# First modulation ahead of the sums of squares, half of the norm's low parts on POOL, and other shares and rounds in the mixing stages

## Chip, cores and metric

One core of a Trainium2 chip runs the whole program. The metric is device time in microseconds of one execution. PE is the matmul engine, DVE, ACT and POOL the three engines for elementwise work, SP the queue that issues most DMAs.

## What is computed

A two-layer backbone of a diffusion model over 256 context and 1024 latent tokens, width 1024. Per layer, cut to what matters:

```
mod = silu(c) @ ada_w[i] + ada_b[i]          # six parts of 1024: shift, scale, gate, twice; a latent and a context row
h   = rmsnorm(x, norm1_g[i]) * (1 + sc1) + sh1
z   = h @ w_in[i]                            # columns for S5, RWKV-7, retention, GLA
mix = concat(s5(z), rwkv7(z), ret(z), gla(z)) @ w_out[i]     # each scans forward and backward
x   = x + g1 * mix
h   = rmsnorm(x, norm2_g[i]) * (1 + sc2) + sh2
x   = x + g2 * (relu(h @ mlp_w1[i]) ** 2 @ mlp_w2[i])
```

## The kernel before, in words

**Matmuls.** Big products are split: each operand is a rounded high part and a low part (the rest), and a product is high × high, high × low and low × high. So each normed tile has a high part `hh` and a low part `hl` (`mh`, `ml` ahead of the output projection and the MLP), and each weight tile `w_hi` and `w_lo`. `Pe.matmul` (L161) records every matmul, so they all have that line. PE takes its instructions in the order in which they were issued, as every engine does.

**Blocks.** The 1280 tokens are three blocks, of 256 (context), 512 and 512 columns, taken in the order 1, 2, 0 (`BORDER`). Each is eight tiles `kt` of 128 rows.

**Start.** `layer` (L1605) for layer 0 loads the three blocks `x`, one DMA each. For each it runs `sumsq`: ACT and POOL square four tiles each (`n_q`), DVE adds them up in `n_qa` (one buffer), PE adds over the rows by a product with ones. Then `rstd`: DVE's `n_s`, logarithm and exponential on ACT with a table load each, and four DVE operations that refine the root `n_r`. Behind all three runs `ada` for the first part: 16 loads of 512 KB (`ada_w`, five buffers), 32 products with the two condition rows, four copies on ACT (`ada_r`), four transposes, and the sum `mod` on DVE. `modg` makes the scale.

**Norm.** `norm` (L1571 on) then makes for each tile `n_h` on DVE (L1580, three buffers), `hh` on ACT with the shift added (L1581) and `hl` on DVE (L1582). It serves norm1 of both layers and the norms ahead of the MLPs. The output projection's inputs are split at L1669 to L1675, where odd tiles' `ml` is already subtracted on POOL.

**Mixing stage.** Behind the projections and S5, three generators run merged: ada's remaining parts, RWKV, and retention followed by GLA. `merged` (L2004) asks the one whose PE cost so far, divided by its share, is least for its next step. The shares are `MW`: the first number, times the number of ada parts (three in layer 0, two in layer 1), is ada's, the second RWKV's, the third that of retention and GLA. The order in which steps are issued, with the framework's scheduler behind it, gives each engine's order.

RWKV works through ten pairs of chunks per layer (`Rwkv.run`, L635). Pair by pair, its first part makes products and stores them (`rw_TE`, `rw_TO` to `rw_S`, L514), loads them in another layout (`rw_B`, one buffer, L518), and inverts unit triangular blocks on POOL in 31 steps of two operations (`rw_tmp` L527, `rw_Yv` L528). The result goes to DRAM and back (L530, `rw_DT` L533) and the second part (`unit2`) uses it. `RL` holds two numbers per layer: a new pair starts every R rounds, and the second part of a pair comes LAT rounds after its first:

```
R, LAT = self.RL
while act or r <= R * (NCH - 1) + LAT:
    b, q = divmod(r - LAT, R)
```

GLA works chunk by chunk; for each, POOL makes 16 scaled copies `gl_L` (L807 to L810), which PE multiplies.

Of the kernel before, what the change touches and what calls it, by code (L numbers as in the profile page):

```python
# [7 lines left out]
F32 = mybir.dt.float32  # L8
F32R = mybir.dt.float32r
I32 = mybir.dt.int32  # L10
AF = mybir.ActivationFunctionType
OP = mybir.AluOpType
# [299 lines left out]
class Rwkv:  # L312
# [268 lines left out]
    def chain(self, u, act):  # L581

        k, nc = self.k, self.k.nc
        V, A, PE = nc.vector, nc.scalar, k.pe
        p, d, ES = u["p"], u["d"], u["ES"]
        need = p >= 2 or self.need_ctx
        Y = self.w.tile([128, 256], F32, name="rw_Y", bufs=3)
        for e in range(2):
            py = k.ps("ch")
            RHi, RHn = self.RH[d, e], self.RH[d, 1 - e]  # L590
            for h in range(4):
                PE.matmul(py[:, h * 64:h * 64 + 64], ES[:, e, h], RHi[:, h], start=True, stop=True)
            y3 = py[:, 0:256].rearrange("p (h v) -> p h v", h=4)
            st = slice(0, 64) if e == 0 else slice(64, 128)
            ys = slice(64, 128) if e == 0 else slice(0, 64)
            yt = slice(0, 64) if e == d else slice(64, 128)
            V.tensor_tensor(RHn[st], y3[st], bc(u["E"][st, :, None], [64, 4, 64]), op=OP.mult)
            if need:
                A.copy(Y[yt], py[ys, 0:256])
            yield  # L600
        if need:
            if p in self.seen:
                act.append([self.finish(p, Y), 0])
            else:
                nc.sync.dma_start(self.dY[p, :, 0], Y)
                self.seen.add(p)
# [28 lines left out]
    def run(self):  # L635


        R, LAT = self.RL
        order = [(p, (1 - p) if p < 2 else (11 - p)) for p in range(NCH)]
        pairs, act, r = [], [], 0  # L640
        while act or r <= R * (NCH - 1) + LAT:
            b, q = divmod(r - LAT, R)
            if q == 0 and 0 <= b < NCH:
                act += [[self.unit2(u, act), 0] for u in pairs[b]["us"]]
            b, q = divmod(r, R)
            if q == 0 and b < NCH:
                pairs.append(dict(n=b, us=[]))
                act += [[self.unit1(order[b][d], d, pairs[b]), 0] for d in range(2)]
            r += 1
            for a in list(act):  # L650
                if a[1] > 0:
                    a[1] -= 1
                    continue
                try:
                    a[1] = next(a[0]) or 0
                except StopIteration:
                    act.remove(a)
                yield
            for pr in pairs:
                if len(pr["us"]) == 2 and "DT" not in pr["us"][0]:  # L660
                    pr["us"].sort(key=lambda u: u["d"])
                    self.inv(pr)
# [782 lines left out]


BLK = ((0, 256), (256, 768), (768, 1280))
MW = ((8, 165, 60), (8, 165, 60))
RL = ((6, 11), (6, 11))
FG = ((1, 4, 7), (2, 5))  # L1450
LATB = (1, 2)
BORDER = (1, 2, 0)
# [6 lines left out]
class Net:  # L1459
# [110 lines left out]
    def norm(self, x, n, g, sh, cond, hh, hl, pool, r=None):  # L1570

        k, nc = self.k, self.k.nc
        if r is None:
            ps = self.sumsq(x, n, pool)
            yield
            r = self.rstd(ps, n, pool)
        for kt in range(8):
            h = pool.tile([128, 512], F32, name="n_h", bufs=3)[:, :n]
            b = sh[:, kt, cond:cond + 1]
            nc.vector.scalar_tensor_tensor(h, x[:, kt], g[:, kt, cond:cond + 1], r[:, :n], op0=OP.mult, op1=OP.mult)  # L1580
            nc.scalar.activation(hh[:, kt], h, AF.Identity, bias=b)  # L1581
            nc.vector.scalar_tensor_tensor(hl[:, kt], h, b, hh[:, kt].bitcast(F32), op0=OP.add, op1=OP.subtract)  # L1582
        yield

    def hblocks(self, pool, name, bs=BORDER):
# [14 lines left out]
    def layer(self, i):  # L1600
        k, nc, I = self.k, self.k.nc, self.I
# [7 lines left out]
        h = self.hblocks(hp, "h")  # L1609
# [3 lines left out]
        npool = self.pool(tag + "n", "right")  # L1613
        if i == 0:
            aw = self.pool("aw", "right")
            self.x, self.nr = [None] * 3, {}
            ad = self.ada(0, 0, aw, 5)
            for b in BORDER:
                c0, c1 = BLK[b]
                self.x[b] = npool.tile([128, 8, c1 - c0], F32, name=f"x0{b}")  # L1620
                nc.sync.dma_start(self.x[b], self.xd[b])
                self.nr[b] = self.rstd(self.sumsq(self.x[b], c1 - c0, npool, 2, 2), c1 - c0, npool, 3)
            run(ad)
            aw.release()
        g1 = self.modg(sm["n1"], mod[:, 8:16])
        for b in BORDER:
# [2 lines left out]
        if i > 0:  # L1629
# [16 lines left out]
                  self.brow(w, "rw_lnb", I["rw_ln_b"][i]), w, not last, self.mixout(w, "rw", 2))  # L1646
        rw.RL = RL[i]
        rw.setup()
        ad = [(i, 1), (i, 2)] + ([] if last else [(i + 1, 0)])
        aw, rww, rgw = MW[i]  # L1650
        merge(k, [(chain([self.ada(a, q, w, 2) for a, q in ad]), aw * len(ad)), (rw.run(), rww), (chain([self.ret_run(i, last), self.gla_run(i, last)]), rgw)])
# [8 lines left out]
        npool = self.pool(tag + "n2", "right")  # L1660
# [4 lines left out]
        for b in ob:  # L1665
            c0, c1 = BLK[b]
            n = c1 - c0
# [11 lines left out]
        h = mix  # L1679
        for b in ob:  # L1680
            n = BLK[b][1] - BLK[b][0]
# [338 lines left out]
def merge(k, gens):  # L2020
    run(merged(k, gens))
# [41 lines left out]
```

## Time and profile before

| | |
|---|---|
| median of 3 runs | 3906.94 us (3906.47 to 3907.89) |
| profiled execution | 3916.12 us, its span 3914.3 us, mean granted clock 0.927 |
| busy: PE, DVE, ACT, POOL | 3563.0, 2254.2, 1476.7, 1350.4 us |
| share of the span's chain: PE, DVE, DMA, POOL, ACT | 67, 10, 8, 7, 5% |

The kernel runs through stages one after the other: start and norm1 to 102 us, projections and S5 to 466, the mixing stage to 1056, output projection and MLP to 2106, and in the same sequence layer 1: norm1 to 2142, projections to 2498, mixing to 3046, the rest to 3914. In the MLPs PE is busy all the time; in the mixing stages every engine has gaps. Busy time of an engine counts only in a stage in which others wait for it.

### The profile page before, as it was taken

The page shows a single profiled execution, that of the slowest core. Times are in us where ns is not written, and L with a number is a line of the kernel's source. Part 1 is how long each engine was busy: PE and PEld are TensorE (multiplying, and loading weights), DVE is VectorE, ACT ScalarE, POOL GpSimd, SP SyncE. Part 2 cuts the span into 40 slices and gives each one's busy share as a digit, 9 for nine tenths or more (in the row PEclk, how much of TensorE's full clock was granted, in tenths as well). Part 3 has the DMA queues.
Part 4 walks back from the last instruction along what each step waited for, and adds up shares of the span by engine and source line. Part 5 has one row for each costly group of instructions (what it writes and reads, how often), then busy time and mean ns, then how long its engine had stood idle before and what let it go on. Part 6 is the DMA issues. An engine that isn't in the chain of part 4 may idle for free.

```text
span 3914.3 us, 61529 instructions
## 1 busy us (share of the span) xinstructions
PE 3563.0 (91%) x23156; PEld 2970.4 (76%) x23156; DVE 2254.2 (58%) x4722; ACT 1476.7 (38%) x2992; POOL 1350.4 (34%) x2697
## 2 busy tenths in 40 slices
PE   3999888988799999999997999898888799999996
PEld 1998756677687888888886887767777678888885
DVE  5876455677565444444447875555776564444446
ACT  3266334765433111211124266446664331112222
POOL 1541156676441111111111551276674421111122
PEclk9999988877799999999998999997877899999998
DMA  4445475632431111111103434563423411111111
GB/s 173 142 127 148 136 216 140 193 85 70 140 113 33 33 44 33 44 33 44 33 28 102 148 120 143 175 210 102 112 76 96 134 59 49 44 43 44 54 49 44
DMA packets 350873, 372.84 MB, mean 95 GB/s; under 512 B 75408, under 2 KB 295760, under 8 KB 350320
## 3 DMA queue, kind: packets, MB, share of 16 engines
q1 hardware_dynamic: 315232, 343.07, 29.1%
q10 hardware_dynamic: 35344, 25.83, 2.2%
q8 instruction: 183, 3.00, 0.3%
q14 instruction: 114, 0.93, 0.1%
HBM read 285.18 MB, written 83.63 MB: 94 GB/s over the span
## 4 chain that ended last, share of the span: by engine, by line
PE 67%; DVE 10%; DMA 8%; POOL 7%; ACT 5%; issue 3%; SPq 1%; ACTq 0%; DVEq 0%; POOLq 0%
PE psb L161 57%; PE psu L161 5%; POOL rw_tmp L527 2%; DMA ada_w<-in_ada_w_dram 2%; POOL rw_Yv L528 2%; DMA rw_B<-rw_S 2%; PE psfi L161 1%; PE pss L161 1%; DVE s_W L1157 1%; DVE n_qa L1552 1%; DMA rw_S<-rw_Yv 1%; PE psch L161 1%; PE psu L165 1%; DVE s_CA L1157 1%; DMA n_h<-z_mix 1%
## 5 line engine op out<-in xcount | busy, mean ns | idle before, releaser
L161 PE MATMUL psb<-hl,w_hi 128*128 128x512 f32 (+1 forms) x1800 | 665.8, 370 | 6.9 <-DVE hl L1582 6.9
L161 PE MATMUL psb<-hh,w_hi 128*128 128x512 f32 (+1 forms) x1800 | 666.0, 371 | 5.3 <-DVE n_s L1561 2.3
L161 PE MATMUL psb<-hh,w_lo 128*128 128x512 f32 (+1 forms) x1800 | 662.6, 369 | 0.0
L161 PE MATMUL psb<-mh,w_hi 128*128 128x512 f32 (+1 forms) x1616 | 604.3, 375 | 21.9 <-ACT w_hi L1475 21.9
L161 PE MATMUL psb<-mh,w_lo 128*128 128x512 f32 (+1 forms) x1616 | 599.1, 372 | 4.1 <-DVE w_lo L1478 3.6
L161 PE MATMUL psb<-ml,w_hi 128*128 128x512 f32 (+1 forms) x1616 | 601.8, 373 | 0.0
L1939 DVE SCALAR_TENSOR_TENSOR x<-psb,mod,x 128x512 f32<-128x512 f32 (+1 forms) x648 | 438.9, 689 | 271.3 <-PE psb L161 270.6
L1478 POOL TENSOR_TENSOR w_lo<-w_raw,w_hi 128x1024 fp32r<-128x1024 f32 x84 | 216.8, 2581 | 751.8 <-ACT w_hi L1475 632.1
L1961 DVE TENSOR_TENSOR hr<-hr 128x512 f32<-128x512 f32 (+1 forms) x162 | 151.7, 937 | 504.6 <-ACT hr L1960 504.6
L1960 ACT ACTIVATE hr<-psb 128x512 f32<-128x512 f32 (+1 forms) x162 | 88.7, 548 | 850.9 <-PE psb L161 850.6
L161 PEld LDWEIGHTS psb<-hl,w_hi 128*128 128x128 f32 x1800 | 342.1, 190 | 72.5 <-DVE hl L1582 12.7
L161 PEld LDWEIGHTS psb<-hh,w_hi 128*128 128x128 f32 x1800 | 342.2, 190 | 67.5 <-issue 4.0
L161 PEld LDWEIGHTS psb<-hh,w_lo 128*128 128x128 f32 x1800 | 341.5, 190 | 59.1 <-issue 0.7
L1963 POOL TENSOR_TENSOR hl<-hr,hh 128x512 fp32r<-128x512 f32 (+1 forms) x81 | 95.6, 1181 | 800.3 <-ACT hh L1962 527.8
L161 PEld LDWEIGHTS psb<-mh,w_hi 128*128 128x128 f32 x1616 | 306.8, 190 | 81.8 <-ACT w_hi L1475 23.1
L161 PEld LDWEIGHTS psb<-mh,w_lo 128*128 128x128 f32 x1616 | 306.8, 190 | 63.1 <-DVE w_lo L1478 5.0
L161 PEld LDWEIGHTS psb<-ml,w_hi 128*128 128x128 f32 x1616 | 306.9, 190 | 58.8 <-issue 1.8
L1475 ACT CAST w_hi<-w_raw 128x1024 fp32r<-128x1024 f32 (+1 forms) x208 | 212.9, 1042 | 274.2 <-PE psb L161 263.0
L527 POOL TENSOR_TENSOR rw_tmp<-rw_Yv,rw_B 128x60 f32<-128x60 f32 (+24 forms) x620 | 206.2, 333 | 185.8 <-DMA rw_B<-rw_S 98.6
L161 PE MATMUL psb<-w_lo,hh 128*128 128x256 f32 (+1 forms) x928 | 264.6, 286 | 1.8 <-DVE w_lo L1478 1.8
L161 PE MATMUL psb<-w_hi,hl 128*128 128x256 f32 (+1 forms) x928 | 264.2, 286 | 0.0
L161 PE MATMUL psb<-w_hi,hh 128*128 128x256 f32 (+1 forms) x928 | 263.5, 288 | 0.3 <-ACT w_hi L1475 0.3
(470 smaller groups left out, 6690.8 us busy)
## 6 DMA issues: line engine op xcount, KB each, us to landing
w_raw<-in_mlp_w_dram SPq DMA_DIRECT2D x128, 512.0 KB
ada_w<-in_ada_w_dram SPq DMA_DIRECT2D x96, 512.0 KB
w_raw<-in_w_in_dram SPq DMA_DIRECT2D x40, 512.0 KB
w_raw<-in_w_out_dram SPq DMA_DIRECT2D x32, 512.0 KB
rw_zin<-z_rw SPq DMA_DIRECT2D x20, 576.0 KB
rw_B<-rw_S SPq DMA_DIRECT2D x20, 512.0 KB
z_rw<-zm SPq DMA_DIRECT2D x14, 640.0 KB
x<-in_xT_dram SPq DMA_DIRECT2D x4, 2048.0 KB
```

Source lines behind the costliest of these rows:

```text
L161: return self.t.matmul(out, lhsT, rhs, **kw)
L165: return self.t.transpose(out, a, ident)
L527: eng.tensor_tensor(o, bc(Yv[:, 0:m, s:s + 1], [128, m, n]), bc(B[:, s:s + 1, s + 1:32], [128, m, n]), op=OP.mult)
L528: eng.tensor_tensor(Yv[:, 0:m, s + 1:32], Yv[:, 0:m, s + 1:32], o, op=OP.add)
L1157: T_ = lambda o, a, b, op: V.tensor_tensor(o, a, b, op=op)
L1475: nc.scalar.copy(hi[:, :n], raw[:, :n])
L1478: e.tensor_tensor(lo[:, :n], raw[:, :n], hi[:, :n].bitcast(F32), op=OP.subtract)
L1552: nc.vector.tensor_tensor(acc[:, :n], acc[:, :n], q[:, :n], op=OP.add)
L1939: V.scalar_tensor_tensor(xb[:, dt_], ps[:, :n], mod[:, 40 + dt_, cnd:cnd + 1], xb[:, dt_], op0=OP.mult, op1=OP.add)
L1960: A.activation(r[:, :n], ps[:, :n], AF.Relu)
L1961: V.tensor_tensor(r[:, :n], r[:, :n], r[:, :n], op=OP.mult)
L1963: (G if j else V).tensor_tensor(hl[:, j, :n], r[:, :n], hh[:, j, :n].bitcast(F32), op=OP.subtract)
```

## The change

Four edits.

1. `MW`: ada's share per part is 16, where it was 8, in both layers.
2. `RL`: a new pair of RWKV chunks starts every 5 rounds, where it was every 6; the second part stays 11 rounds behind.
3. `norm`: for odd tiles ACT adds the shift in place, ACT copies the high part, and POOL subtracts to get the low part. Even tiles stay as they were. In the whole program 88 tiles are normed by it, 64 of 512 columns and 24 of 256.
4. `layer`: for layer 0 the three blocks' loads are followed by ada's first part, and by the sums and roots of the three blocks behind it.

```diff
-MW = ((8, 165, 60), (8, 165, 60))
-RL = ((6, 11), (6, 11))
+MW = ((16, 165, 60), (16, 165, 60))
+RL = ((5, 11), (5, 11))
...
-            nc.scalar.activation(hh[:, kt], h, AF.Identity, bias=b)
-            nc.vector.scalar_tensor_tensor(hl[:, kt], h, b, hh[:, kt].bitcast(F32), op0=OP.add, op1=OP.subtract)
+            if kt % 2:
+                nc.scalar.activation(h, h, AF.Identity, bias=b)
+                nc.scalar.copy(hh[:, kt], h)
+                nc.gpsimd.tensor_tensor(hl[:, kt], h, hh[:, kt].bitcast(F32), op=OP.subtract)
+            else:
+                nc.scalar.activation(hh[:, kt], h, AF.Identity, bias=b)
+                nc.vector.scalar_tensor_tensor(hl[:, kt], h, b, hh[:, kt].bitcast(F32), op0=OP.add, op1=OP.subtract)
...
-                self.nr[b] = self.rstd(self.sumsq(self.x[b], c1 - c0, npool, 2, 2), c1 - c0, npool, 3)
             run(ad)
+            for b in BORDER:
+                n = BLK[b][1] - BLK[b][0]
+                self.nr[b] = self.rstd(self.sumsq(self.x[b], n, npool, 2, 2), n, npool, 3)
```

PE's order at the start of the program, before (a row is an engine's instruction with its line, what it writes and reads, and how often it stands there in a row; `psb` is a bank of PSUM):

```order
L161 MATMUL psb_107<-n_qa,c_ones 128x512
L161 MATMUL psb_144<-n_qa,c_ones 128x512
L161 MATMUL psb_181<-n_qa,c_ones 128x256
L161 MATMUL psb_216<-ada_w,condsl 2x512 x32
L165 MATMUL psb_287<-c_ident,ada_r 128x128 x4
L161 MATMUL psb_425<-hh_92,w_hi 128x512
```

And with the change:

```order
L161 MATMUL psb_111<-ada_w,condsl 2x512 x32
L165 MATMUL psb_182<-c_ident,ada_r 128x128 x4
L161 MATMUL psb_188<-n_qa,c_ones 128x512
L161 MATMUL psb_223<-n_qa,c_ones 128x512
L161 MATMUL psb_258<-n_qa,c_ones 128x256
L161 MATMUL psb_437<-hh_92,w_hi 128x512
```

The three sums over rows moved from ahead of ada's products to behind its transposes.

DVE's order around the modulation of layer 0 (`mod`), before, with the last of the third block's sum and root chain (`n_qa` to `n_r`) ahead of it:

```order
L1552 TENSOR_TENSOR n_qa<-n_qa,n_q_200 128x256
L1561 TENSOR_SCALAR n_s<-psb_181 128x256
L1564 TENSOR_TENSOR n_t<-n_r 128x256
L1565 TENSOR_TENSOR n_t<-n_t,n_s 128x256
L1566 TENSOR_SCALAR n_t<-n_t 128x256
L1567 TENSOR_TENSOR n_r<-n_r,n_t 128x256
L1531 TENSOR_TENSOR mod_75<-psb_287,small_73 128x32
L1539 SCALAR_TENSOR_TENSOR modg<-mod_75,small_73 128x16
L1580 SCALAR_TENSOR_TENSOR n_h<-x_105,modg,n_r 128x512 x3
L1582 SCALAR_TENSOR_TENSOR hl_93<-n_h,mod_75,hh_92 128x512 x2
```

And with the change, from the last add of the first block on:

```order
L1552 TENSOR_TENSOR n_qa<-n_qa,n_q_207 128x512
L1478 TENSOR_TENSOR w_lo<-w_raw,w_hi 128x1024 x3
L1531 TENSOR_TENSOR mod_75<-psb_182,small_73 128x32
L1539 SCALAR_TENSOR_TENSOR modg<-mod_75,small_73 128x16
L1561 TENSOR_SCALAR n_s<-psb_188 128x512
L1552 TENSOR_TENSOR n_qa<-n_qa,n_q_225 128x512
L1552 TENSOR_TENSOR n_qa<-n_qa,n_q_229 128x512
L1564 TENSOR_TENSOR n_t<-n_r 128x512
L1552 TENSOR_TENSOR n_qa<-n_qa,n_q_230 128x512
L1565 TENSOR_TENSOR n_t<-n_t,n_s 128x512
L1552 TENSOR_TENSOR n_qa<-n_qa,n_q_235 128x512
L1566 TENSOR_SCALAR n_t<-n_t 128x512
```

All three root chains, and the second and third block's adds, moved from ahead of the modulation to behind it, in between the norm's operations.

POOL's order at the end of the last inversion of layer 0, before (`gl_L` are a GLA chunk's copies, `rw_Y` to `gl_nth` the outputs' group norms):

```order
L809 TENSOR_TENSOR gl_L<-gl_c 128x8x8
L810 TENSOR_TENSOR gl_L<-gl_c 128x8x8
L528 TENSOR_TENSOR rw_Yv<-rw_Yv,rw_tmp 128x7x4
L527 TENSOR_TENSOR rw_tmp<-rw_Yv,rw_B 128x24
L528 TENSOR_TENSOR rw_Yv<-rw_Yv,rw_tmp 128x8x3
L527 TENSOR_TENSOR rw_tmp<-rw_Yv,rw_B 128x16
L528 TENSOR_TENSOR rw_Yv<-rw_Yv,rw_tmp 128x8x2
L527 TENSOR_TENSOR rw_tmp<-rw_Yv,rw_B 128x8
L528 TENSOR_TENSOR rw_Yv<-rw_Yv,rw_tmp 128x8
L624 TENSOR_TENSOR rw_Y<-rw_Y,rw_YQ 128x256
```

And with the change:

```order
L527 TENSOR_TENSOR rw_tmp<-rw_Yv,rw_B 128x8
L528 TENSOR_TENSOR rw_Yv<-rw_Yv,rw_tmp 128x8
L624 TENSOR_TENSOR rw_Y<-rw_Y,rw_YQ 128x256
L706 TENSOR_TENSOR rw_grs<-rw_gs,mhalf 128x4
L706 TENSOR_TENSOR gl_nrs<-gl_ns,mhalf 128x4
L624 TENSOR_TENSOR rw_Y<-rw_Y,rw_YQ 128x256
L706 TENSOR_TENSOR rw_grs<-rw_gs,mhalf 128x4
L724 TENSOR_TENSOR gl_nth<-gl_nth,gl_lng 128x256
L807 TENSOR_TENSOR gl_L<-gl_c 128x64
L808 TENSOR_TENSOR gl_L<-gl_c 128x64
L809 TENSOR_TENSOR gl_L<-gl_c 128x64
L810 TENSOR_TENSOR gl_L<-gl_c 128x64
```

The last GLA chunk's sixteen copies, which stood inside the inversion, come behind it. In layer 0 eight chunks' copies stood inside inversions and two between them; now six do, three stand between and one behind.

## Rows read from the trace of the kernel before

**Rows 1.** Stretches: each engine's busy us (instructions), PE's granted clock, DMA share, GB/s.

```profile
core 0: us, PE busy (x) PEld busy (x) DVE busy (x) ACT busy (x) POOL busy (x), PEclk, DMA share, GB/s
...
95.00:105.00 10.00, 10.00 (x53) 8.40 (x54) 9.64 (x38) 4.75 (x9) 0.00 (x0) 1.00 0.29 108
...
466.00:1056.00 590.00, 498.13 (x4986) 394.98 (x4986) 392.02 (x1037) 316.97 (x859) 367.64 (x1005) 0.81 0.49 140
1010.00:1037.00 27.00, 27.00 (x382) 24.02 (x386) 14.12 (x33) 9.92 (x25) 3.61 (x5) 0.72 0.15 45
2106.00:2133.00 27.00, 14.34 (x43) 9.85 (x43) 27.00 (x44) 18.39 (x25) 1.44 (x2) 0.68 0.57 175
2498.00:3046.00 548.00, 462.00 (x4438) 379.96 (x4438) 355.40 (x945) 295.78 (x802) 337.85 (x952) 0.79 0.44 129
```

**Rows 2.** PE's timeline, start: start us, length, instruction, count, [idle before, releaser].

```profile
49.13 1.22 PE L161 MATMUL psb<-n_qa,c_ones 128*128 128x256 f32 x2 [11.01 <-DVE n_qa L1552]
50.27 3.73 PE L161 MATMUL psb<-ada_w,condsl 128*2 128x512 f32 x20
...
69.13 1.03 PE L161 MATMUL psb<-ada_w,condsl 128*2 128x512 f32 x4 [0.26 <-DMA ada_w<-in_ada_w_dram]
72.74 1.05 PE L165 MATMUL psb<-c_ident,ada_r 128*128 128x128 f32 x4 [2.58 <-ACT ada_r L1524]
75.83 0.79 PE L161 MATMUL psb<-hh,w_hi 128*128 128x512 f32 x1 [2.03 <-ACT hh L1581]
```

**Rows 3.** DVE's timeline, start.

```profile
24.74 0.69 DVE L1561 TENSOR_SCALAR n_s<-psb 128x512 f32<-128x512 f32 x1 [2.17 <-PE psb L161]
...
33.49 0.68 DVE L1567 TENSOR_TENSOR n_r<-n_r,n_t 128x512 f32<-128x512 f32 x1
...
73.83 0.19 DVE L1531 TENSOR_TENSOR mod<-psb,small 128x32 f32<-128x32 f32 x1 [19.14 <-PE psb L165]
...
100.62 1.27 DVE L1582 SCALAR_TENSOR_TENSOR hl<-n_h,mod,hh 128x256 fp32r<-128x256 f32 x3
```

**Rows 4.** Tile rw_B's readers on POOL, 466 to 1056: ns min/median/max, first, last.

```profile
L527 POOL TENSOR_TENSOR rw_tmp<-rw_Yv,rw_B x310: 201/298/1347, 519.7 to 1003.0; 128x60 f32<-128x60 f32 x15, 128x54 f32<-128x54 f32 x10, 128x66 f32<-128x66 f32 x10, 128x28 f32<-128x28 f32 x10
```

**Rows 5.** POOL's timeline, an inversion of layer 0 and one of layer 1.

```profile
784.11 0.29 POOL L807 TENSOR_TENSOR gl_L<-gl_c 128x64 f32<-128x64 f32 x1 [1.46 <-DMA gl_c<-z_gk]
...
793.01 0.34 POOL L810 TENSOR_TENSOR gl_L<-gl_c 128x64 f32<-128x64 f32 x1
...
2951.90 0.38 POOL L807 TENSOR_TENSOR gl_L<-gl_c 128x64 f32<-128x64 f32 x1 [4.97 <-PE psb L161]
```

**Rows 6.** SP's timeline ahead of the inversion from 768.6 on.

```profile
750.71 0.83 SPq L514 DMA_DIRECT2D rw_S<-rw_TE  x2
...
758.00 0.57 SPq L518 DMA_DIRECT2D rw_B<-rw_S  x1
```

**Rows 7.** ACT's timeline, start.

```profile
12.56 0.63 ACT L1549 ACTIVATE n_qa<-x 128x512 f32<-128x512 f32 x1 [6.41 <-DMA x<-in_xT_dram]
...
24.74 0.63 ACT L1549 ACTIVATE n_qa<-x 128x512 f32<-128x512 f32 x1 [2.30 <-PE psb L161]
```

**Rows 8.** DVE in 2106 to 2133, by line: busy us, mean ns.

```profile
L1582 DVE SCALAR_TENSOR_TENSOR hl<-n_h,mod,hh 128x512 fp32r<-128x512 f32 x15 | 10.9, 746 | 0.0
```

**Rows 9.** POOL's timeline at the inputs of layer 0's output projection.

```profile
1063.51 1.26 POOL L1675 TENSOR_TENSOR ml<-n_h,mh 128x512 fp32r<-128x512 f32 x1 [12.30 <-ACT mh L1673]
```

**Rows 10.** DVE's timeline in the same place.

```profile
1062.79 0.69 DVE L1675 TENSOR_TENSOR ml<-n_h,mh 128x512 fp32r<-128x512 f32 x1 [10.65 <-ACT mh L1673]
1064.15 1.17 DVE L1675 TENSOR_TENSOR ml<-n_h,mh 128x512 fp32r<-128x512 f32 x1 [0.67 <-ACT mh L1673]
```

**Rows 11.** The page's costliest groups: busy us, mean ns, idle before.

```profile
L161 PE MATMUL psb<-ml,w_hi 128*128 128x512 f32 (+1 forms) x1616 | 601.8, 373 | 0.0
```

**Rows 12.** PE in 1010 to 1037, groups by line.

```profile
L161 PE MATMUL psb<-gl_L 32*32 32x32 f32 (+1 forms) x228 | 7.3, 222 | 0.0
```

**Rows 13.** Waits in 466 to 1056: total us, times, longest.

```profile
PE psfi L161 <- DMA ada_w<-in_ada_w_dram: 15.1, 5, 7.2
```

## The prediction

> **What bounds the kernel now.** I read the profile in this order: the busy times by stretch, the four engines' timelines at the start, the two norms, the POOL chain of the two mixing stages, and last the order of both kernels. The profiled execution took 3916.1 us, 9.2 above the median of the runs, 3906.9. I sum differences against it and carry the sum over to the median. About 0.2%, 7.8 us, is what a measurement can tell from no change.
>
> PE is the engine that counts, and it is short of work in a few places only. In 466 to 1056 and 2498 to 3046, the stages that mix RWKV, retention and GLA, it is busy 498 of 590 and 462 of 548 us; at the second norm1 it has 14.3 us of work in 27 while DVE is busy all of them [rows 1]. At the start it stands in order: its first ada matmul comes at 50.27, right behind the third sum of squares, and the first twenty then run without a wait, so five loads had been there for long. The other eleven follow at 1.29 us each to 69.13; transposes at 72.74, first projection at 75.83 [rows 2]. DVE sat idle for 19.1 us before the modulation at 73.83 and ends the norm at 101.9 [rows 3]. From 95 on PE has no gap [rows 1].
>
> The mixing stages hang on a chain on POOL: twenty inversions of 31 steps each, where the next pair's block is loaded into the one buffer that the last one frees. Ten of them run from 519.7 to 1003 in layer 0, some 48 us each, though a step is two operations of 0.3 us, some 20 us in all [rows 4]. The rest is the load, and other POOL work that stands between the steps. Two GLA chunks inside one inversion took 784.1 to 793.3, some 4.2 us each without the steps between, and in layer 1 the chain stood 5 us behind a GLA operation that waited for PE [rows 5]. The RWKV products that feed the load are there 7 us before it is issued [rows 6].
>
> **Start (ada's first part ahead of the sums).** No operation is removed. The x blocks' loads, 5 MB, are first on SP, then 16 ada loads with 5 of weights among them, 10.5 MB: 31 halves of a megabyte at 1.29 us, 40 us. The first 2 MB were there at 12.56 [rows 7], so the stream began at about 7.4 and the last ada load is there at 47. Its transposes end 4.7 us later, as now [rows 2], at 52, against 73.8. ACT's copies of ada's result and DVE's modulation now stand behind three casts and three low parts of weights; the loads of those are issued ahead of the eleventh ada load, so they are over by then. But now PE runs the three sums behind them. The buffer of sums is one: the second block's first square waits for the first sum on PE, as now at 24.74 [rows 7]. So the second and third sums and their root chains move behind the modulation, where the wait for ada hid them. From a sum's n_s to its n_r DVE and ACT need 9.4 us [rows 3]; the first normed tile starts at about 63, 11 us earlier than now.
>
> The norm's end decides, as PE takes the three blocks in turn. From 63 on DVE has 16 n_h and 8 hl of 512 columns at 0.73 [rows 8], 17.5; 12 of 256 at 0.42 [rows 3], 5; the third block's adds, 3; two root chains of five operations, 5: 30 us, or an end at 93. POOL has 8 subtracts of 1.26 [rows 9], four of half the size, 2.5, and four squares, 2.5: 15 us. If DVE stands still for all of those, the end is 108.
>
> Does it stand still? A subtract on DVE of two SBUF tiles took 0.69 alone and 1.17 when it started 0.64 us into a POOL subtract; it ended 0.55 after that one [rows 9, 10], so it lost 0.48 of the 0.62 us that POOL still needed, some 80%. Taken so, the norm ends at 63 + 30 + 12 = 105. PE has been running gapless since 95 on what was done, so some 3 us more than now cost nearly nothing: **+1 us, between −10 (no standstill) and +4 (full standstill)**.
>
> The Trainium skill (SBUF — State Buffer, "Who interferes with whom") speaks against this part of the change: a VectorE instruction with two SBUF inputs and a GpSimd one that reads SBUF share a port pair, and the second one waits for the whole instruction. By it the start would be +4 and the next term +4, the sum 5 us higher; the 1.17 us row agrees with a wait, a little short of a full one.
>
> **norm1 of layer 1 (the same subtracts).** DVE is the bound for the two large blocks, 27 of 27 us [rows 1]. A pair of tiles costs it 4 × 0.73 = 2.92 [rows 8]. With the odd subtract on POOL it is 2.19 with no standstill, 2.19 + 1.26 = 3.45 with a full one, 3.20 at 80%. Eight pairs: −6, +4, and I take **+2**. ACT's three operations of a pair, one more than now, take 1.9 us at the 0.63 of its square [rows 7], less than DVE's. The three n_h buffers hold: by these prices an odd tile keeps its own for 3.3 us and an even one for 2.1, together 1.8 us a pair. The norms ahead of the MLP cost **0**, ±2: no matmul ever waits for ml [rows 11], because the other blocks' work covers them; if that cover went, each would pay the 2 us of above.
>
> **Shares and rounds (the mixing stages).** Both edits only reorder. In POOL's order of layer 0, GLA chunks inside inversions go from 8 to 6: pair 5 loses both (−8.4 at 4.2 each [rows 5], and a wait), pair 6 gains one, pair 8 loses one, pair 4 gets small ones. Where a chunk stands while the load is under way it costs nothing. By pairs I get −10 for the chain; with the waits it could be −16, and if the moved work only makes others late 0. But one chunk's work now comes after the last inversion, and PE has 271 GLA matmuls instead of 162 behind its last pair. There it is busy 27 of 27 us at a granted clock of 0.72 [rows 1], 7.3 us of them on gl_L products alone [rows 12]; two thirds more of these and their like is +8. Net **−2**, from −14 to +12. In layer 1 one chunk leaves the second last inversion, −4.2 and perhaps the 5 us wait [rows 5], others move by a few us either way, and the tail is as before: **−4**, from −12 to +6. The ada loads come denser and all ahead of pair 4. PE's waits for them are 15.1 us in the whole stage [rows 13], ahead of products that are 7 us early: 0, within the ends above.
>
> **Sum.** +1 + 2 − 2 − 4 = −3: 3904 us. All lower ends together would be −44, all upper +28; they hardly meet.
>
> **Rivals.**
> *No standstill worth the name.* The 1.17 us may be one unlucky pair. Then the start gives −10 and norm1 −6, with −6 from the mixing stages: −22, 3885. For it: DVE was the one engine at work in both norms. Against it: the row itself.
> *The tails don't fill.* The clock of 0.72 rises to the 1.00 of other stretches and the extra GLA products fit in; the chains give −10 and −6, norms +3: −13, 3894.
> *Slower: the GLA backlog behind layer 0's last pair.* If the chain's end at 1003 doesn't come earlier, since the chunks taken out of inversion 5 return in 6 and 7, the +8 stays whole, and the last chunk's scores, their mask and norm on DVE follow in series, some 8 more; with +5 from the norms and −2 from layer 1 it is +19, 3926. It decides once the last inversion ends less than 8 us earlier. For it: PE is full there. Against: two chunks less in the chain.
> *The change does nothing where POOL bounds.* The load and the 31 steps are the same; then only the norms' +3 count: 3910, within the forecast's own case.
>
> **Chances.** Forecast with the last rival 0.38, no standstill 0.19, tails that fill 0.16, backlog 0.20, and 0.07 for larger losses of the same kind. Of the two faster rivals nearly all is faster by over 0.2% (0.34 after a little is taken off); the backlog and its like and a bit of the forecast give slower 0.28; same 0.38. The range 3880 to 3932 takes in the first rival at its low end and the backlog with 6 us to spare. The forecast's own range is 3897 to 3912.
>
> **What would show it.** Right: the first projection at 63 to 66 but the norm's end near 104; POOL's new subtracts at 1.2 to 1.3 us with n_h or hl beside them lengthened to over 1 us; DVE's stretch of the second norm1 2 us longer; ten inversions ending some 10 us earlier against the stage's start, and the stage shorter by much less. Wrong: a norm that ends at 93, DVE operations at their 0.73 beside POOL, a last inversion of layer 0 as late as now, or a stage that is shortened by all its chain gave.

## The result, and the profile after

The changed kernel took **3925.81 us** (median of 4 runs, 3919.04 to 3929.23), the kernel before 3906.7 beside it: ratio 1.0051, 95% interval 1.0032 to 1.0071. It is slower by 0.5%, where 3904 was forecast. The profiled execution is one of 3926.94 us, span 3925.1.

To compare stages I count PE's matmuls of projections, output projections and MLPs from the start of the program (their order is the same in all kernels here up to a few rows) and read when the n-th starts. "Start" ends at the 200th, layer 0's mixing stage lies between the 2200th and the 2400th, norm1 of layer 1 between the 7300th and the 9000th, layer 1's mixing stage between the 9400th and the 9600th. Two repeats with the identical order of matmuls (`n_dve1` of before, `n1a` of the change, below) give each kernel a second trace:

| us | before | its repeat | changed | its repeat | difference of means |
|---|---|---|---|---|---|
| start, to the 200th | 119.9 | 122.5 | 125.9 | 125.2 | +4.4 |
| layer 0's mixing stage | 647.6 | 640.7 | 644.3 | 642.3 | -0.9 |
| norm1 of layer 1 | 346.3 | 344.2 | 342.4 | 342.2 | -3.0 |
| layer 1's mixing stage | 602.2 | 593.9 | 610.0 | 605.9 | +9.9 |
| last matmul | 3893.1 | 3884.5 | 3903.3 | 3899.7 | +12.7 |

The other +2.3 are small parts of the MLPs and projections. Before's profiled execution, 9 us over its median, was long in the mixing stages: its repeat, with the same order, is 15.2 us shorter in these two and 6.6 longer elsewhere, 8.6 shorter in sum. "norm1 of layer 1" is a long stretch, since the end of layer 0's MLP lies in it too.

PE's timeline at the start of the changed kernel (columns as in [rows 2]):

```profile
48.86 1.03 PE L161 MATMUL psb<-ada_w,condsl 128*2 128x512 f32 x4 [1.74 <-DMA ada_w<-in_ada_w_dram]
52.47 1.09 PE L165 MATMUL psb<-c_ident,ada_r 128*128 128x128 f32 x4 [2.58 <-ACT ada_r L1524]
53.35 1.92 PE L161 MATMUL psb<-n_qa,c_ones 128*128 128x512 f32 x2
68.38 2.08 PE L161 MATMUL psb<-n_qa,c_ones 128*128 128x512 f32 x2 [13.12 <-DVE n_qa L1552]
84.11 1.22 PE L161 MATMUL psb<-n_qa,c_ones 128*128 128x256 f32 x2 [13.65 <-DVE n_qa L1552]
87.25 0.77 PE L161 MATMUL psb<-hh,w_hi 128*128 128x512 f32 x1 [1.92 <-DVE n_s L1561]
```

DVE's timeline there, and POOL's:

```profile
53.60 0.19 DVE L1531 TENSOR_TENSOR mod<-psb,small 128x32 f32<-128x32 f32 x1 [13.16 <-PE psb L165]
65.67 2.06 DVE L1580 SCALAR_TENSOR_TENSOR n_h<-x,modg,n_r 128x512 f32<-128x512 f32 x3
77.28 1.75 DVE L1580 SCALAR_TENSOR_TENSOR n_h<-x,modg,n_r 128x512 f32<-128x512 f32 x1
96.87 0.74 DVE L1580 SCALAR_TENSOR_TENSOR n_h<-x,modg,n_r 128x512 f32<-128x512 f32 x1
106.25 0.47 DVE L1587 SCALAR_TENSOR_TENSOR hl<-n_h,mod,hh 128x256 fp32r<-128x256 f32 x1
```

```profile
77.04 1.44 POOL L1584 TENSOR_TENSOR hl<-n_h,hh 128x512 fp32r<-128x512 f32 x1
```

The modulation comes at 53.6 (73.83 in [rows 3]) and the first normed tile at 65.67. But the first projection starts at 87.25, later than the 75.83 of [rows 2]: the sums of the second and third block stand ahead of it on PE, and it waits for them 13.1 and 13.7 us. The norm ends at 106.7 (101.9 before).

The stretches of the mixing stages and of the second norm1 (columns as in [rows 1]):

```profile
466.00:1060.00 594.00, 495.12 (x5018) 393.26 (x5016) 390.83 (x1037) 317.51 (x860) 364.15 (x1004) 0.81 0.47 133
2108.00:2135.00 27.00, 11.34 (x35) 8.63 (x36) 26.54 (x36) 18.67 (x27) 10.26 (x8) 0.62 0.47 141
2498.00:3056.00 558.00, 450.69 (x4452) 369.06 (x4450) 355.16 (x945) 298.13 (x802) 339.62 (x951) 0.80 0.45 127
```

In the mixing stages busy times are those of [rows 1] within 3%; what grew is idle time. In the second norm1 POOL has 10.3 us of work in place of 1.4, and DVE is still busy for 26.5 of 27. The inversions (tile rw_B's readers on POOL, as in [rows 4]) span 480.6 us in layer 0 (483.3 before) and 473.8 in layer 1:

```profile
L527 POOL TENSOR_TENSOR rw_tmp<-rw_Yv,rw_B x310: 201/296/1422, 527.1 to 1007.7; 128x60 f32<-128x60 f32 x15, 128x54 f32<-128x54 f32 x10, 128x66 f32<-128x66 f32 x10, 128x28 f32<-128x28 f32 x10
L527 POOL TENSOR_TENSOR rw_tmp<-rw_Yv,rw_B x310: 202/297/2487, 2549.8 to 3023.6; 128x60 f32<-128x60 f32 x15, 128x54 f32<-128x54 f32 x10, 128x66 f32<-128x66 f32 x10, 128x28 f32<-128x28 f32 x10
```

In before the same tile gives 451.8 for layer 1:

```profile
L527 POOL TENSOR_TENSOR rw_tmp<-rw_Yv,rw_B x310: 198/297/2707, 2548.0 to 2999.8; 128x60 f32<-128x60 f32 x15, 128x54 f32<-128x54 f32 x10, 128x66 f32<-128x66 f32 x10, 128x28 f32<-128x28 f32 x10
```

Why, shows at the last pair of layer 1. POOL ended the inversion before it at 2971.8, and SP stored the pair's products at 2978.77 only, and loaded them at 2982.16; POOL began at 2992.82. POOL's timeline:

```profile
2971.63 0.21 POOL L528 TENSOR_TENSOR rw_Yv<-rw_Yv,rw_tmp 128x8 f32<-128x8 f32 x1
...
2992.82 0.24 POOL L527 TENSOR_TENSOR rw_tmp<-rw_Yv,rw_B 128x31 f32<-128x31 f32 x1 [12.62 <-issue]
```

and SP's:

```profile
2978.77 0.81 SPq L514 DMA_DIRECT2D rw_S<-rw_TE  x2
2980.00 0.80 SPq L514 DMA_DIRECT2D rw_S<-rw_TO  x2
2982.16 0.58 SPq L518 DMA_DIRECT2D rw_B<-rw_S  x1
```

In the repeat of before the same store is issued 8 us ahead of the inversion's end, which lets the load go at 2958.90:

```profile
2951.10 0.81 SPq L517 DMA_DIRECT2D rw_S<-rw_TE  x2
...
2958.90 0.56 SPq L521 DMA_DIRECT2D rw_B<-rw_S  x1
```

I call the time from the end of an inversion to the issue of the next pair's load a **late store**: where it is long, as here, the buffer is free and the products are not stored. Summed over the ten pairs of layer 1 it is 2.7 and 3.9 us in before and its repeat, 16.8 and 14.3 in the changed kernel and its. As I read it, the products were late since PE waited elsewhere. PE's waits of 2500 to 3056 have a row for it, the second here, which is not among before's longest (where rw_DT stands first as well):

```profile
PE psu L161 <- DMA rw_DT<-rw_S: 26.1, 5, 9.0
PE psb L161 <- DVE gl_nq L725: 13.7, 4, 5.9
```

`gl_nq` waits for a root that POOL makes in between an inversion's steps, so POOL's chain holds up PE, which holds up POOL's next pair. No run takes one of these waits away, so this chain is read from the trace and not shown. PE's waits for ada's loads in the same stretch, which the prediction put at 0, grew from 6.7 and 6.4 us (before and its repeat) to 13.7 and 13.8; they don't decide the stage alone, as m_pool4 below has 15.2 us of them, with the old shares, in a stage of 603.5.

### The profile page after: what moved, and what is told of

It reads as the page before. It is cut to its first block, busy times and chain, and to the rows that moved or that the text cites. A ratio compares the mean times of both kernels' runs of the same rounds, so it can differ in the third digit from the quotient of the medians.

```text
span 3925.1 us, 61600 instructions
## 1 busy us (share of the span) xinstructions
PE 3547.0 (90%) x23156; PEld 2957.0 (75%) x23156; DVE 2252.4 (57%) x4678; ACT 1501.4 (38%) x3040; POOL 1394.9 (36%) x2741
## 5 line engine op out<-in xcount | busy, mean ns | idle before, releaser
L161 PEld LDWEIGHTS psb<-hh,w_lo 128*128 128x128 f32 x1800 | 342.2, 190 | 59.7 <-issue 0.5
```

The source lines that it names most:

```text
L161: return self.t.matmul(out, lhsT, rhs, **kw)
```

## The experiments

First, the kernel before with one part of the change each:

- `e1_order`: only the start's order (edit 4 of the diff).
- `e2_norm`: only the norm's odd tiles (edit 3).
- `e3_rounds`: `RL = ((5, 11), (5, 11))`.
- `e4_share`: `MW = ((16, 165, 60), (16, 165, 60))`.

> The kernel before with the new order of the start alone. Theory A (PE's place in order): PE's first projection now stands behind all three sums of squares, of which the third ends some 30 us after the modulation, so the first projection comes near 85 us where it was at 75.8, the norm ends at 103 to 107, and the run is 4 to 7 us slower. Rival B (POOL's subtracts are what eats the start's gain): the order alone gains, first projection near 65 and 6 to 10 us faster.

> The kernel before with the odd tiles' low parts on POOL alone. Theory A: the ends of both norm1 move by under 3 us either way, since what DVE saves it mostly stands still for; the second norm1 gains some 2 us; total -4 to +2. Rival B (full standstill): both norm1 end 4 us later, total +6 to +9. Rival C (no standstill): both end 5 us earlier, total -10.

> The kernel before with a new RWKV pair every 5 rounds and the old shares. Theory A (the rounds make the loss in layer 1's mixing stage): layer 1's last inversion ends 10 us or more later against the stage's start, with the last pairs' stores after the inversion before them has ended, and the run is 8 to 15 us slower. Rival D (the shares make it): within 4 us of before.

> The kernel before with ada's share at 16 and the old rounds. Theory A: within 4 us of before, ada's loads 50 us earlier at their end in layer 0 and nothing waiting for it. Rival D: layer 1's mixing stage is 8 us or more longer, through PE's waits for ada's loads ahead of the RWKV products.

| part alone | median us | ratio (95%) | start | layer 0's stage | layer 1's stage |
|---|---|---|---|---|---|
| start's order | 3947.99 | 1.0101 (1.0081 to 1.0120) | 125.5 | 685.3 | 600.0 |
| POOL subtracts | 3966.02 | 1.0147 (1.0124 to 1.0169) | 128.2 | 666.4 | 630.0 |
| rounds | 3942.20 | 1.0097 (1.0079 to 1.0115) | 122.8 | 653.9 | 622.4 |
| shares | 3972.65 | 1.0157 (1.0130 to 1.0184) | 120.3 | 669.7 | 619.9 |

All four totals missed by far (e1's own start, 5.6 us longer, was within what I expected), and the parts don't add: alone they cost 36 to 66 us each, together 19. The start's order alone touches nothing behind the first norm and gives the start the changed kernel's 125.5, but layer 0's stage grows by 38. The reason is in the order of instructions. The kernel opens its context with `schedule_with_timeline_sim=True` (L2059): the framework lays each engine's order by a modelled timeline. With the start's order alone 697 of the 2858 rows of matmuls of layer 0's mixing stage stand elsewhere, and 471 of the 2570 of layer 1's (rows outside the longest common order; projections and MLPs keep theirs). So a new theory: **the plan**. Any edit that shifts the modelled times draws a new order of both mixing stages, and a stage's time is that of the order drawn. Idle edits test it.

```diff
 m_pool4 (on before), a_pool4 (on the change): at the begin of each mixing stage
+        pad = w.tile([128, 64], F32, name="pad", bufs=1)
+        for _ in range(4):
+            nc.gpsimd.memset(pad, 0.0)
 i1 (on before), i_a (on the change): the start
-                self.nr[b] = self.rstd(self.sumsq(...
+            for b, steps in zip(BORDER, (7, 5, 3)):
+                for _ in range(steps):
+                    next(ad)
+                n = BLK[b][1] - BLK[b][0]
+                self.nr[b] = self.rstd(self.sumsq(self.x[b], n, npool, 2, 2), n, npool, 3)
             run(ad)
```

> Kernel before with four idle memsets of 128x64 on POOL (1 us of work in all) at the begin of each mixing stage. The order of layer 0's matmuls is the same as before's, row by row; in layer 1's mixing stage 226 to 382 of each 500 matmul rows stand elsewhere, though nothing in the program's work differs. Theory re-planning (the scheduler lays both mixing stages anew after any shift, and before's plan was one with hardly a late store): layer 0's mixing stage within 3 us of before; layer 1's longer by 8 to 30 us, with POOL's wait for a store that is not there (buffer free, products late) at 10 to 37 us over the ten pairs, where before has 2.7; total +8 to +30. Rival (a plan is as good as another, the edits themselves cost what the single parts cost): both stages and the total within 4 us of before.

> The changed kernel with the same four memsets. Matmul order the same up to layer 1's mixing stage, 235 to 400 of each 500 rows elsewhere in it. Theory re-planning: start, first norm and layer 0 within 3 us of the changed kernel (so it also repeats the start's +6 at the 200th projection matmul); layer 1's mixing stage differs from it by 5 to 25 us, either way, and the late stores of layer 1 (16.8 us in the changed kernel) differ with it. Rival (rounds of 5 and shares of 16 cost layer 1 its 8 us): layer 1's stage within 4 us of the changed kernel.

> Kernel before with one difference at the start: ada's steps are issued in between the sums (PE: 2 ada products, first sum, 14, second sum, 8, third sum, 8, transposes) so that no sum stands behind the modulation and no ada product waits for the third sum. Theory (the changed start loses since PE's first projection stands behind all three sums): the modulation at 53 to 57 against 73.8, first projection at 56 to 62 against 75.8 and 87.2, 200th projection matmul 12 to 18 us ahead of before's. Rival (the start is bound by loads or by DVE, whose norm follows anyway): 200th within 5 us of before. Both mixing stages are laid anew; by the theory of re-planning they cost 0 to 45 us more than before's, so the total is -15 to +30; if plans cost nothing, it is -12 to -18.

> The changed kernel with the same interleaved start in place of its own, the other three parts kept. Theory: 200th projection matmul 12 to 20 us ahead of the changed kernel's (POOL's subtracts then overlap the sums' squares less); total -10 to -20 against it if the plans of the mixing stages were equally good, which the theory of re-planning leaves open by 30 us either way. Rival (loads or DVE bind the start): 200th within 5 us of the changed kernel's.

| | median us | ratio (95%) | start | layer 0's stage | layer 1's stage |
|---|---|---|---|---|---|
| m_pool4 | 3915.38 | 1.0027 (1.0015 to 1.0039) | 120.8 | 641.7 | 603.5 |
| a_pool4 | 3937.86 | 1.0089 (1.0065 to 1.0113) | 126.2 | 646.8 | 625.1 |
| i1 | 3935.14 | 1.0080 (1.0064 to 1.0097) | 104.2 | 670.4 | 617.3 |
| i_a | 3924.69 | 1.0048 (1.0029 to 1.0066) | 108.9 | 662.9 | 614.2 |

The first form of the theory, that before's plan is the best and any other costs 8 us or more, fell: with 570 rows of layer 1 elsewhere, m_pool4 has 603.5 there. A plan is a draw, good or bad. On the changed kernel the same four memsets cost layer 1 15 to 19 us (625.1 against 610.0 and 605.9).

The interleaved start did what was expected of it. PE's timeline in i1:

```profile
22.37 1.87 PE L161 MATMUL psb<-ada_w,condsl 128*2 128x512 f32 x4 [22.37 <-DMA ada_w<-in_ada_w_dram]
24.18 2.08 PE L161 MATMUL psb<-n_qa,c_ones 128*128 128x512 f32 x2
...
50.12 1.22 PE L161 MATMUL psb<-n_qa,c_ones 128*128 128x256 f32 x2 [4.59 <-DVE n_qa L1552]
51.27 3.59 PE L161 MATMUL psb<-ada_w,condsl 128*2 128x512 f32 x16
57.47 0.63 PE L165 MATMUL psb<-c_ident,ada_r 128*128 128x128 f32 x4 [2.61 <-ACT ada_r L1524]
60.14 0.79 PE L161 MATMUL psb<-hh,w_hi 128*128 128x512 f32 x1 [2.04 <-ACT hh L1581]
```

With no sum behind the transposes the first projection comes at 60.1 and the start is 15.7 us shorter than before's. With POOL's subtracts (i_a) it is 11.0 shorter: there they cost the start 4.7. Both lost it again in layer 0's stage.

The third set: 64 one-column memsets on DVE at setup (`n_dve64`), edits 3 and 4 together (`x_12`), the interleaved start with ada's share 7 (`i1w_7`), and the same with rounds of 5 and shares of 16 (`i_34`).

> Kernel before with 64 idle one-column memsets on DVE at setup, before the first input is there. No work, share or round differs. The order of matmuls is the same up to layer 0's mixing stage; in it 240 to 421 of each 500 matmul rows stand elsewhere, in layer 1's 270 to 408. Theory re-planning (where a shift makes the scheduler lay a stage anew, the new plan's time is drawn from a spread as wide as the single parts showed): start within 5 us of before; layer 0's mixing stage (from the 2200th projection matmul to the output projection's first) 5 to 40 us longer than before's 617.4, layer 1's (from the 9400th to the 9600th) within -3 to +26 of before's 602.2. Rival (plans cost nothing, the parts' edits did): both stages and the total within 5 us of before.

> The start's order and the POOL subtracts together, shares and rounds as before. Start as in the changed kernel by every theory: first projection at 86 to 89, 200th projection matmul +5 to +7. Norm1 of layer 1 (7300th to 9000th) -2 to -5 against before, as in the other kernels with subtracts on POOL. Theory re-planning: the mixing stages are whatever the new plan gives, -5 to +40 in layer 0 and -3 to +26 in layer 1, with no relation to e1's +38 or e2's in layer 0. Rival (parts add): layer 0's stage is +38 or more, as with the start's order alone, and layer 1's +20 or more, as with the subtracts alone.

> The interleaved start on the kernel before, with ada's share 7 in place of 8, for another plan of both mixing stages. Start as with the interleaved start alone: first projection at 60, 200th at 104 (-15.7). Theory re-planning: layer 0's mixing stage anywhere from 617 to 655, where the interleaved start alone had 639; layer 1's 599 to 628; total -18 to +45 against before. Rival (an earlier start is always paid back in layer 0, since something else bounds it): layer 0's stage again 635 to 643.

> The changed kernel with the interleaved start and with the norm's low parts left on DVE. Start: 200th projection matmul at 104 (-15.7 against before), 4.7 ahead of the same with POOL's subtracts, if those cost the start DVE time; at 109 if they don't. Norm1 of layer 1: 0 to -2 against before, where POOL's subtracts gave -4. Layer 0: with rounds of 5 and shares of 16 RWKV runs ahead of GLA, and GLA's last copies end at 1069 to 1075 whatever the start; theory (GLA's own backlog bounds the stage): again 1065 to 1076 with the last inversion ending 40 us or more before the last GLA product; rival (it was the plan's chance): GLA's end moves with the start, to 1050 to 1060.

| | median us | ratio (95%) | start | layer 0's stage | layer 1's stage |
|---|---|---|---|---|---|
| n_dve64 | 3919.64 | 1.0020 (1.0005 to 1.0035) | 121.3 | 640.6 | 597.2 |
| x_12 | 3947.49 | 1.0099 (1.0079 to 1.0119) | 126.0 | 668.2 | 610.3 |
| i1w_7 | 3926.05 | 1.0046 (1.0032 to 1.0060) | 103.8 | 668.7 | 616.6 |
| i_34 | 3923.93 | 1.0034 (1.0021 to 1.0046) | 104.2 | 671.5 | 610.9 |

n_dve64 drew no new plan, against what I expected of it (240 to 421 of each 500 rows elsewhere, and 5 to 40 us more): in both mixing stages its trace has the instructions of PE, DVE, ACT and POOL in before's order, one by one. So it doesn't say what a new plan costs; it is a third trace of before's order, with 640.6 and 597.2 us (m_pool4's layer 0 is a fourth, with 641.7). x_12 shows that parts don't add: 668.2 and 610.3, where its parts alone had 685.3 and 666.4, 600.0 and 630.0. In i_34 ACT's last operation on GLA's output starts at 1075.0 us, in i_a at 1071.0, in the changed kernel at 1069.2, as i_34's expectation had it; that the last inversion ended 10 and 22 us earlier in these two than the changed kernel's 1008.2 brought nothing. For these three orders GLA's own backlog is thus as good a reading of the stage's end as the draw.

What was open then was the repeatability, whether layer 1's numbers matter, and whether layer 0 pays back any early start. `x_a60` is the changed kernel with `MW` 8 and `RL` 6 in layer 1; n_dve1 and n1a have one idle memset at setup; `i1w_10` is the interleaved start with share 10.

> Kernel before with one idle one-column memset at setup: the order of matmuls is the same row by row in the whole program, so this repeats before. Theory (before's profiled execution was a slow sample of its own, by 9 us, in the mixing stages): median within 4 us of before's; stages at the start, projections and MLPs within 2 us of before's trace; layer 0's mixing stage 640 to 645 (2200th projection matmul to the 2400th matmul, which lies in the output projection; before 647.6) and layer 1's (9400th to 9600th) 595 to 602 (before 602.2). Rival (the 9 us lie outside what the trace holds): both stages as in before's trace within 2 us.

> The changed kernel with the same idle memset, the same order row by row: repeats the changed kernel. Median within 4 us of its 3925.8; first projection at 87 to 89, layer 0's stage 642 to 648 (644.2 there), layer 1's 606 to 614 (610.0). If layer 1's comes out under 604, its +7.7 was chance of one execution and not of the kernel.

> The changed kernel with rounds and share of layer 1 as before (6 and 8); layer 0 keeps the changed numbers and its order row by row. Theory plan: layer 1's stage is drawn anew, between 597 and 630, not put right by the old numbers; start and layer 0 as in the changed kernel within 4 us. Rival (rounds of 5 and shares of 16 cost layer 1 its 7.7): layer 1's stage back to 600 to 604, the total 6 to 9 us under the changed kernel's.

> The interleaved start on the kernel before with ada's share 10, for a plan of layer 0 far from the others. Start: 200th projection matmul at 104 (-15.7). Theory plan: layer 0's stage (2200th to 2400th) anywhere from 640 to 685; total -16 to +40 against before. Rival (what the start gains is paid back in layer 0, since another thing bounds its end): the 2400th matmul again at 1102 to 1117, as in the four kernels with this start so far, however early the stage begins.

| | median us | ratio (95%) | start | layer 0's stage | layer 1's stage |
|---|---|---|---|---|---|
| n_dve1 | 3913.42 | 1.0019 (1.0007 to 1.0031) | 122.5 | 640.7 | 593.9 |
| n1a | 3928.29 | 1.0060 (1.0039 to 1.0081) | 125.2 | 642.3 | 605.9 |
| x_a60 | 3945.71 | 1.0104 (1.0089 to 1.0119) | 126.1 | 647.3 | 629.8 |
| i1w_10 | 3931.26 | 1.0064 (1.0050 to 1.0077) | 103.6 | 676.9 | 610.9 |

An unchanged order repeats a stage within 9 us in a trace. The medians of n_dve1 and n_dve64, both with before's order, lay 6 and 12 us over before's (I expected 4 at most for n_dve1), and both intervals leave out 1; so a difference of 0.2 to 0.3% between two kernels here says nothing yet. The changed kernel and its repeat, with 19 and 21 us, lie beyond it. With before's own rounds and share in layer 1, x_a60 is 20 us longer there than the changed kernel: the numbers are not what layer 1 lost by. With a_pool4, whose four memsets alone moved the stage by 15 us or more, that leaves the plan.

Last, the plan against the start. `d4` is the kernel before with four idle multiplications ahead of the scale of layer 0, under 1 us; its plan of layer 0 is that of i1 but for 49 rows. `i1d8` has the interleaved start and eight of them.

```diff
         g1 = self.modg(sm["n1"], mod[:, 8:16])
...
+        if i == 0:
+            for _ in range(4):
+                nc.vector.tensor_scalar(mod[:, 8:16], mod[:, 8:16], 1.0, None, op0=OP.mult)
```

> Kernel before with four idle multiplications by one of 128x8 on DVE ahead of the scale of layer 0 (under 1 us). Its plan of layer 0 is the interleaved start's but for 49 of 2900 matmul rows, its start is before's. Theory plan: layer 0's stage (2200th to 2400th) 662 to 672, as with the interleaved start (670.4) and with the POOL subtracts alone (666.4, a plan that differs in 59 rows), against 640.7 to 647.6 of before's plan; start +0 to +2; total +15 to +45 with layer 1 drawn anew. Rival (the stage is longer because the start was earlier, since something else bounds its end): layer 0's stage 640 to 648.

> Interleaved start with eight such idle multiplications (under 1.5 us): layer 0's plan differs from the interleaved start's in 516 of 2900 rows and from before's in 470. Start: 200th projection matmul at 104 to 106. Theory plan: layer 0's stage 640 to 680, not tied to 670; total -18 to +35 against before. Rival (paid back): the 2400th matmul at 1110 to 1120 again.

| | median us | ratio (95%) | start | layer 0's stage | layer 1's stage |
|---|---|---|---|---|---|
| d4 | 3949.35 | 1.0102 (1.0084 to 1.0120) | 120.9 | 670.2 | 617.3 |
| i1d8 | 3931.72 | 1.0059 (1.0046 to 1.0073) | 105.6 | 666.4 | 616.0 |

**d4 settles it for this plan.** Its stage took 670.2, i1's 670.4, e2's (59 rows from i1's) 666.4, though the stage began 17 us later in d4 than in i1, and 25 in e2; with before's plan it takes 641 to 648. Under 1 us of idle work made the kernel 1% slower. The traces of d4 and i1 repeat each other in detail. POOL's timeline in d4, where a GLA chunk's copies stand around the first step of an inversion and wait 9.75 us with it for the load:

```profile
816.14 0.47 POOL L808 TENSOR_TENSOR gl_L<-gl_c 128x64 f32<-128x64 f32 x1
826.36 0.24 POOL L527 TENSOR_TENSOR rw_tmp<-rw_Yv,rw_B 128x31 f32<-128x31 f32 x1 [9.75 <-DMA rw_B<-rw_S]
826.56 0.29 POOL L809 TENSOR_TENSOR gl_L<-gl_c 128x64 f32<-128x64 f32 x1
```

and in i1:

```profile
803.19 0.29 POOL L808 TENSOR_TENSOR gl_L<-gl_c 128x64 f32<-128x64 f32 x1
813.01 0.24 POOL L527 TENSOR_TENSOR rw_tmp<-rw_Yv,rw_B 128x31 f32<-128x31 f32 x1 [9.53 <-DMA rw_B<-rw_S]
813.21 0.29 POOL L809 TENSOR_TENSOR gl_L<-gl_c 128x64 f32<-128x64 f32 x1
```

Of fourteen different orders of layer 0 two took under 650 us (before's and the changed kernel's, each in four traces), the others 654 to 685. No kernel beat before: the interleaved start, worth 11 to 16 us, met a longer layer 0 in all six draws. That this is the plan and not the start's own doing is shown for i1's plan only (by d4); i1w_10 and i1d8, whose 2400th matmul comes at 1120.9 and 1112.6, fit either expectation nearly as well, so for the other five it is open. What makes a plan good is read, not proved, too: late stores sum to 1.3 to 6.2 us in layer 0 of the four traces of before's order, but to 42.6 in e1 and 40.2 in i1w_10, while i1 and d4 have few (4.6 and 3.6) and lose by longer inversions (398.9 and 398.1 us in sum, 382.4 in before). And half of what these two lose lies behind the mixing proper: from the output projection's first matmul to the 2400th they take 56.0 and 56.1 us, before and its repeat 41.4 and 42.2. There PE waits once more for a weight that ACT casts, in i1 (7.23 us in d4):

```profile
1080.87 0.80 PE L161 MATMUL psb<-mh,w_hi 128*128 128x512 f32 x1 [7.03 <-ACT w_hi L1475]
```

The granted clock of that stretch is 0.82 in i1 and 0.85 in d4, against 0.96 in before and its repeat. e2 takes 58.7 us there.

## Why the prediction was wrong, point by point

**Start: +1 forecast, +4.4 measured, outside its own ends.** The modulation (52 forecast, 53.6), the first normed tile (63, 65.7) and the norm's end (104 to 105, 106.7) were right within 3 us. The step that failed is "the first projection at 63 to 66". I had the order before me, with three sums between the transposes and the first projection, and priced their root chains on DVE but not PE's wait for them. PE began at 87.25 with all of the first blocks' work still to do, and had too much left when the norm ended. i_a, which is the changed kernel with the sums taken from that place and nothing else, has the first projection at 60.1 and a start 17.0 us shorter.

**Standstill of DVE: right in kind.** In the start an n_h of 0.74 took 1.75 when it began 0.24 us into a subtract of 1.44: it lost 1.01 of the 1.20 us that POOL still needed, 84% where [rows 9, 10] gave 77% (0.48 of 0.62, put as some 80% in the prediction). By the Trainium skill (SBUF — State Buffer, "Who interferes with whom") it would have lost all 1.20; as before, the trace is a little short of the rule. In i_a against i1 it costs the start 4.7 us. In the changed kernel itself the subtracts cost the start next to nothing (x_12 126.0, e1 125.5): PE has its work late there and is busy for 38.1 of the 39 us from 87 to 126.

**norm1 of layer 1: +2 forecast, -3.0 measured, not told apart from 0.** DVE from 2104 to 2136 in the changed kernel, by line and shape (busy us, mean ns):

```profile
L1580 DVE SCALAR_TENSOR_TENSOR n_h<-x,modg,n_r 128x512 f32<-128x512 f32 x14 | 12.5, 926 | 0.0
L1587 DVE SCALAR_TENSOR_TENSOR hl<-n_h,mod,hh 128x512 fp32r<-128x512 f32 x6 | 6.5, 1076 | 0.5 <-ACT hh L1586 0.5
```

and in before from 2102 to 2136, where `hl` takes 746 on average as in [rows 8]:

```profile
L1580 DVE SCALAR_TENSOR_TENSOR n_h<-x,modg,n_r 128x512 f32<-128x512 f32 x16 | 12.1, 778 | 0.0
```

A pair of tiles now costs 2 × 0.926 + 1.076 = 2.93, not the 3.20 of the forecast and a little less than the 2 × (0.778 + 0.746) = 3.05 of before: POOL's subtracts (mean 1.49) cost DVE less than the 80% of their time that I took. Eight pairs make 1 us of this. The whole stretch is 340.7 to 343.0 us in e1, e3 and e4 too, which have no subtracts on POOL, so the rest of the -3 is not shown to be theirs.

**Layer 0: -2 forecast, -0.9 measured, with other terms.** The inversions became shorter by 6 to 8 us in sum (376.5 and 375.8 against 382.4 and 383.5, and not 10), but late stores took it back (11.1 and 10.3 against 6.2 and 2.6). And the tail's +8 hardly came: behind the last pair PE does work on GLA until 1067, as forecast, but in before it had stood idle there for a weight that ACT casts. PE's first row of the output projection in the repeat of before, and then in the changed kernel:

```profile
1061.06 0.79 PE L161 MATMUL psb<-mh,w_hi 128*128 128x512 f32 x1 [13.31 <-ACT w_hi L1478]
```

```profile
1067.05 0.66 PE L165 MATMUL psb<-c_ident,gl_nq 128*128 128x128 f32 x2 [5.02 <-DVE gl_nq L726]
1069.58 0.79 PE L161 MATMUL psb<-mh,w_hi 128*128 128x512 f32 x1 [1.86 <-ACT gl_mix L1727]
```

So the rival "the GLA backlog behind layer 0's last pair" named the right time, 3926, for a wrong reason: its condition held (against the stage's start the last inversion ended 1.2 us earlier, in the repeats 0.4), its backlog was there, and it filled a gap. Its price counted +5 for the norms, where the forecast has +3, and 16 for layer 0, where nothing came. That the range to 3932, which was drawn around this rival, holds the measured time is luck.

**Layer 1: -4 forecast with ends of -12 and +6, +9.9 measured.** This term is the one that turned the sign. "One chunk leaves the second last inversion, -4.2 and perhaps the 5 us wait": the inversions' sum stayed (366.5 and 365.6 against 366.4 and 364.1), and late stores made 10 to 14 of the 17 to 21 us by which the last inversion ended later against the stage's start; the tail won part of it back. I took the products as 7 us early from one place of layer 0 [rows 6], and priced the chunks that moved as if the rest of the order stayed. It did not: 560 of 2570 rows of PE stand elsewhere in that stage. By a_pool4 and x_a60 the loss isn't the rounds' or shares' own: with the new numbers four orders of the stage took 606 to 625, with before's numbers nine took 594 to 630. What can be said of this change is that it drew a good order in layer 0 and a middling one in layer 1. The error was thus one of the range's making as well: a term for the draw, by these runs up to +45 us in layer 0 and +36 in layer 1, was missing, and with it a chance of 0.34 for faster had no ground.

## What to carry to other kernels

Where the order is laid by a modelled timeline, compare the whole program's order, not the edited place: an edit that shifts a stage by under 1 us can redraw a later one and cost 1%, so run the edit beside idle edits before its time is credited to it. At the start of a pipeline, look at what stands on the consuming engine between the producer and the first use; an early result behind two late ones in the same queue is a late result. Read the bound of a chain from all its links: here the load could only go when the buffer was free and the products were stored, and I had priced one of the two.

## What was not expected of the hardware

Two executions of the same order of matmuls differed by 8.6 us in the trace (before and n_dve1), with granted clocks of 0.927 and 0.932. Over the four traces of before's order layer 0's mixing stage lies between 640.6 and 647.6 us, and layer 1's in three of them between 593.9 and 602.2; the projections of layer 0 (340 us) agree within 0.4 us, and the stretch from the 2400th matmul to the 7300th (970 us) within 2.6. In these traces the stages in which PE has gaps are also the ones whose time repeats worst.
